# Encoder block with a mixture of experts: the last stage's row sums moved to TensorE, its one-hots to GpSimd

## Chip, cores and metric

One core of a Trainium2 chip runs the whole kernel. The metric is device microseconds of one execution, taken as the median of three runs. "us" below is microseconds and "span" is the time from the first to the last instruction in a profiled execution. PE is TensorE (the matrix engine), DVE is VectorE, ACT is ScalarE, POOL is GpSimd and SP is SyncE, which here only issues DMAs.

## What is computed

The block is a normalised input projection, two mixers (Fourier and state space), a gated output projection, and then a mixture of 64 experts with two experts for each of 2048 rows of 1024 numbers. Only the end of it matters for this change:

```python
def _rmsnorm(x, g):
    inv = lax.rsqrt(jnp.mean(x * x, axis=-1, keepdims=True) + RMS_EPS)
    return x * inv * g

# x: 2048 x 1024, after the two mixers
hn = _rmsnorm(x, ffn_norm_g)
# each row goes to two of 64 experts: a = silu(xb @ w_gate[e]) * (xb @ w_up[e]); y = (a @ w_down[e]) * weight
x = x + hier_moe(hn, ...)          # sum of the row's two weighted expert results
return _rmsnorm(x, final_norm_g)
```

All of it is float32. Products of large matrices are made of three products of a high and a low part in a reduced format (`fp32r`), so every weight block is first split into two parts `w_h` and `w_l`.

## The kernel before

The kernel goes through stages one after another; the expert loop (`stage_e`) takes 64 experts, one 128-row tile each, and the last stage (`stage_z`) puts the results together. In the expert loop ACT and DVE split each 128x2048 block of weights (L1685 and L1691), PE multiplies, and each expert's result rows are scattered by GpSimd to `y01` in memory. `y01` has two halves of 2048 rows: half 0 holds the row's residual plus its first expert's result, half 1 its second expert's result. The results of the last two experts, 62 and 63, are not scattered. They stay on the chip as pairs of parts in `r_last` (written by `last_result` at L1795, L53 and L54), and the last stage adds them into their rows by a product with a one-hot matrix: `oh` has a one where a row's number in the tile equals the number of a result row (`col`), so `oh` times the result places each result row where it belongs.

The last stage covers the 2048 rows in 16 tiles of 128 rows, in `steps`: seven steps of two tiles and then two steps of one. For step `n`, `load` brings the two halves of `y01` into `ys[n, 0]` and `ys[n, 1]` on SP's queue (L1992). The stage then does this for every step:

- `add(n)`, L2012: GpSimd adds the two halves into `ys[n, 0]`, 128x2048 numbers in one instruction.
- `onehot(n)`, L2020: DVE makes the step's one-hots, two for each tile, one for each of the last two experts.
- `products(n)`, L2032: PE multiplies one-hots and result parts into two PSUM buffers of 128x512 per tile (pools `pgu` with four buffers and `py` with two, so three tiles fit): eight products a tile.
- `total(n)`, L2041 and L2042: DVE adds PSUM to `ys[n, 0]`, two instructions a tile; ACT squares the sum and accumulates the row's mean square.
- `rsqrt_steps`, L72 to L78: DVE scales (L72), GpSimd takes the power -1/2 (L73), and DVE refines it in four small instructions (L75 to L78).
- `final(n)`, L2048: DVE multiplies the sum by the inverse root and by the weight vector `gf`, one instruction a tile.
- `store(n)`, L2052: the result goes out, on GpSimd's queue for the first seven steps and on ACT's for the last two.

These are written in a loop with `products` one step ahead and `onehot` and `add` two steps ahead. No planner moves them: each engine runs its instructions in the order in which the code issues them, and an instruction waits for what it reads. `stage_z` is a generator: `stage_e` runs it up to its first `yield` in expert 62 and up to its second in expert 63, and up to the third after `down(63)`, the last expert's products (L59 to L61 into `py`), and ahead of `last_result(63)`; then it runs to the end.

Of the kernel before, what the change touches and what calls it, by code (L numbers as in the profile page):

```python
# [11 lines left out]
F32 = mybir.dt.float32  # L12
F32R = mybir.dt.float32r
I32 = mybir.dt.int32
AF = mybir.ActivationFunctionType
OP = mybir.AluOpType
# [3 lines left out]
P = 128  # L20
# [16 lines left out]
class K:  # L37
# [1935 lines left out]
    def stage_z(self):  # L1973

        nc, tc, i, mr = self.nc, self.tc, self.i, self.mr
        V, A, SP = nc.vector, nc.scalar, nc.sync
        E = 64
        steps = [(2 * n, 2) for n in range(7)] + [(14, 1), (15, 1)]
        N = len(steps)
        rows = lambda v, t, m: v[t * P : (t + m) * P].rearrange("(t p) d -> p t d", p=P)  # L1980
        ys, tiles, marks, ohs, pss = {}, {}, {}, {}, {}

        def load(n, k, eng):
            t, m = steps[n]
            if n in late:
                tiles[n, k] = self.ewp.tile([P, 2048], F32R, name=("w_h", "w_l")[k]).bitcast(F32)
            elif k < m:
                tiles[n, k], mark = self.raw_tile()
                marks.setdefault(n, []).append(mark)
            both = tiles[n, min(k, m - 1)].rearrange("p (t d) -> p t d", t=2)  # L1990
            ys[n, k] = both if m == 2 else both[:, k : k + 1]
            eng.dma_start(ys[n, k], rows(self.y01, 16 * k + t, m))  # L1992


        late = (5, 6)
        self.ring = self.full
        self.loads += [(lambda eng, n=n, k=k: load(n, k, eng), n not in late and k < steps[n][1]) for n in (0, 1, 2, 3, 4, 7) + late + (8,) for k in range(2)]
        self.load_end = len(self.loads) - 6

        col = mr.tile([P, 2, 16], F32, name="z_col")  # L2000
        idx = mr.tile([P, 2], F32, name="z_idx")
        V.tensor_scalar(idx, self.tb[:, E - 2 : E, 0], 2.0 * T, None, op0=OP.add)
        for q in range(2):
            V.scalar_tensor_tensor(col[:, q], self.iota[:, 0:16], -128.0, idx[:, q : q + 1].to_broadcast([P, 16]), op0=OP.mult, op1=OP.add)
        yield
        g = mr.tile([P, D], F32, name="gf", tag="hn")
        A.dma_start(g, i["final_norm_g"].broadcast_to([P, D]))
        yield

        def add(n):  # L2010
            if n < N:
                nc.gpsimd.tensor_tensor(out=ys[n, 0], in0=ys[n, 0], in1=ys[n, 1], op=OP.add)  # L2012

        def onehot(n):
            if n < N:
                t0, m = steps[n]
                ohs[n] = mr.tile([P, 2, 2, P], F32R, name=f"oh{n % 2}", tag=("hnT", "rw")[n % 2])
                for t in range(m):
                    for q in range(2):
                        V.tensor_scalar(ohs[n][:, t, q], self.iota, col[:, q, t0 + t : t0 + t + 1], None, op0=OP.is_equal)  # L2020

        def products(n):
            if n < N:
                for t in range(steps[n][1]):
                    pool, name = ((self.pgu, "pgu"), (self.pgu, "pgu"), (self.py, "py"))[len(pss) % 3]
                    pss[n, t] = [pool.tile([P, 512], F32, name=name) for h in range(2)]
                    for h in range(2):
                        hs = slice(512 * h, 512 * h + 512)
                        for q in range(2):
                            w = self.r_last[q - 2]  # L2030
                            for k, part in enumerate((w.h, w.l)):
                                nc.tensor.matmul(pss[n, t][h], ohs[n][:, t, q], part[:, hs], start=q + k == 0, stop=q + k == 2)  # L2032

        def total(n):
            y0, y1 = ys[n, 0], ys[n, 1]
            m = steps[n][1]
            ss = mr.tile([P, 2], F32, name="ssz", bufs=2)
            for t in range(m):
                for h in range(2):
                    hs = slice(512 * h, 512 * h + 512)  # L2040
                    V.tensor_tensor(out=y0[:, t, hs], in0=y0[:, t, hs], in1=pss[n, t][h], op=OP.add)  # L2041
                A.activation(y1[:, t], y0[:, t], AF.Square, accum_out=ss[:, t : t + 1])  # L2042
            return self.rsqrt_steps(ss[:, :m], m, *(mr.tile([P, m], F32, name=f"z{m}{n % 2}{q}") for q in "vyt"))

        def final(n, inv):
            y0, y1 = ys[n, 0], ys[n, 1]
            for t in range(steps[n][1]):
                V.scalar_tensor_tensor(y1[:, t], y0[:, t], inv[:, t : t + 1], g, op0=OP.mult, op1=OP.mult)  # L2048

        def store(n):  # L2050
            t0, m = steps[n]
            (nc.gpsimd if n < N - 2 else A).dma_start(rows(self.out, t0, m), ys[n, 1])  # L2052
            for m in marks.get(n, []):
                m[0] = True
            self.load_more()

        add(0)
        add(1)
        onehot(0)
        onehot(1)  # L2060
        yield
        self.load_end = len(self.loads)
        self.load_more()
        products(0)
        for n in range(N):
            products(n + 1)
            norm = total(n)
            if n:
                final(n - 1, inv)
            next(norm)  # L2070
            if n:
                store(n - 1)
            onehot(n + 2)
            add(n + 2)
            inv = next(norm)
        final(N - 1, inv)
        store(N - 1)


# [114 lines left out]
```

## Time and profile before

| what | us |
|---|---|
| median of three runs (2478.20 to 2482.54) | 2479.97 |
| the profiled execution | 2482.89 |
| its span | 2481.1 |
| the last expert's last product starts | 2384.35 |
| first addition of the last stage (L2041) starts | 2389.53 |

The profile is of one execution, 2.9 us above the median. The span of 2481.1 us is 1.8 us less than that execution's whole time. Times in the trace count from the start of the span, so the last stage is the stretch from about 2384 to 2481 us. A timeline row gives the start, the duration, the engine, the line of the kernel and "out<-in" with the names of the tiles; what stands in brackets is the engine's idle time before it and what ended it. Rows of small instructions that follow each other are merged with a count. Busy time of DVE includes time in which an instruction has begun but does not get on. "PEclk" is the clock granted to TensorE, as a share of 2.4 GHz: 1.00 is 2.4 GHz, 0.50 is 1.2 GHz, and a number between is a stretch that held both.

### The profile page before, as it was taken

Reading aid. Unit: us, or ns where it says so; the run is one execution under the profiler, and the core shown is the slowest. Engines: PE = TensorE matmul, PEld = TensorE weight load, DVE = VectorE, ACT = ScalarE, POOL = GpSimd, SP = SyncE. Lnnn points to the kernel's source line nnn. Section 1 sums busy time; section 2 is a strip of 40 time slices with the busy share of each in tenths; the row PEclk is TensorE's granted clock in tenths of the full one; section 3 lists DMA queues with packets and bytes.
Section 4 is the critical chain, followed back from the end, with each engine's and each line's share of the span. In section 5 each row is a group of like instructions: output and inputs, shape, how many; then the busy total and the mean of one; then the engine's idle time right before and its main releaser. Section 6 shows DMA issues by size and latency. Waiting matters only on the chain.

```text
span 2481.1 us, 32354 instructions
## 1 busy us (share of the span) xinstructions
PE 2304.4 (93%) x11770; PEld 1914.1 (77%) x11770; DVE 2111.1 (85%) x2944; ACT 1367.5 (55%) x1635; POOL 722.2 (29%) x354
## 2 busy tenths in 40 slices
PE   6998999999998999996999979999999999999974
PEld 6997778878787999984877768777777777777752
DVE  7786779888936556556999979999999999999998
ACT  4443245544533222223777758777777777777721
POOL 2224500000002010012333231232246556556434
PEclk9999999999999999997999989999999999999985
DMA  5566644364445333346999979999999999989982
GB/s 192 179 192 214 237 129 157 111 229 128 132 123 197 114 108 95 110 142 234 334 342 365 375 270 393 362 352 351 361 356 361 367 365 365 384 318 360 361 316 118
DMA packets 201404, 632.70 MB, mean 255 GB/s; under 512 B 28998, under 2 KB 99656, under 8 KB 150556
## 3 DMA queue, kind: packets, MB, share of 16 engines
q1 hardware_dynamic: 170668, 571.01, 63.7%
q0 software_dynamic: 23104, 47.06, 5.1%
q10 hardware_dynamic: 7472, 12.55, 1.6%
q8 instruction: 93, 1.52, 0.3%
q14 instruction: 67, 0.55, 0.1%
HBM read 560.75 MB, written 103.32 MB: 268 GB/s over the span
## 4 chain that ended last, share of the span: by engine, by line
DVE 41%; PE 36%; issue 12%; DMA 6%; ACT 3%; POOL 1%; SPq 1%; DVEq 0%; POOLq 0%; ACTq 0%
DVE w_l L1691 19%; PE pg L59 3%; PE pg L61 3%; PE pg L60 3%; DVE xT_l L1770 3%; DVE xn L1829 2%; PE po L59 2%; PE pgu L60 2%; PE po L61 2%; PE po L60 2%; PE pgu L61 2%; PE pgu L59 2%; DVE xg L1795 2%; DVE a L1869 2%; ACT w_h L1685 2%
## 5 line engine op out<-in xcount | busy, mean ns | idle before, releaser
L1691 DVE TENSOR_TENSOR w_l<-raw,w_h 128x2048 fp32r<-128x2048 f32 x384 | 875.4, 2319 | 11.9 <-ACT w_h L1685 11.9
L1685 ACT CAST w_h<-raw 128x2048 fp32r<-128x2048 f32 x384 | 726.3, 1906 | 205.4 <-PE pgu L61 164.4
L59 PE MATMUL pgu<-w_h,xT_h 128*128 128x512 f32 x1024 | 406.7, 397 | 14.4 <-issue 14.4
L60 PE MATMUL pgu<-w_l,xT_h 128*128 128x512 f32 x1024 | 406.9, 397 | 4.6 <-DVE w_l L1691 2.3
L61 PE MATMUL pgu<-w_h,xT_l 128*128 128x512 f32 x1024 | 401.8, 392 | 0.0
L1758 POOL DMA_INDIRECT y<-xg,ix x42 | 180.7, 4302 | 423.3 <-DVE aT_l L1770 386.2
L60 PEld LDWEIGHTS pgu<-w_l,xT_h 128*128 128x128 f32 x1024 | 193.8, 189 | 65.3 <-DVE w_l L1691 28.2
L59 PEld LDWEIGHTS pgu<-w_h,xT_h 128*128 128x128 f32 x1024 | 193.7, 189 | 53.5 <-issue 14.6
L61 PEld LDWEIGHTS pgu<-w_h,xT_l 128*128 128x128 f32 x1024 | 193.4, 189 | 39.2 <-DVE xT_l L1770 0.2
L59 PE MATMUL pg<-hk_h,wg_h 128*128 128x512 f32 x512 | 206.6, 404 | 6.8 <-ACT gt_t L834 6.5
L59 PE MATMUL py<-w_h,aT_h 128*128 128x512 f32 x512 | 206.0, 402 | 4.0 <-ACT aT_h L1768 4.0
L61 PE MATMUL pg<-hk_h,wg_l 128*128 128x512 f32 x512 | 201.6, 394 | 1.8 <-DVE wg_l L54 1.8
L60 PE MATMUL pg<-hk_l,wg_h 128*128 128x512 f32 x512 | 201.0, 393 | 0.0
L61 PE MATMUL py<-w_h,aT_l 128*128 128x512 f32 x512 | 200.9, 392 | 0.0
L60 PE MATMUL py<-w_l,aT_h 128*128 128x512 f32 x512 | 200.9, 392 | 0.0
L1758 POOL DMA_INDIRECT y<-x_l,ix x22 | 94.4, 4292 | 235.6 <-DVE aT_l L1770 228.2
L1753 POOL DMA_INDIRECT xg<-x,ix x42 | 156.9, 3735 | 12.8 <-issue 12.8
L59 PEld LDWEIGHTS pg<-hk_h,wg_h 128*128 128x128 f32 x512 | 97.2, 190 | 27.9 <-ACT gt_t L834 7.1
L61 PEld LDWEIGHTS pg<-hk_h,wg_l 128*128 128x128 f32 x512 | 97.1, 190 | 23.6 <-DVE wg_l L54 2.7
L54 POOL TENSOR_TENSOR w_out_l<-raw_hn,w_out_h 128x1024 fp32r<-128x1024 f32 x1 | 2.4, 2377 | 386.6 <-DMA raw_x_l<-in_w_out 386.6
L59 PEld LDWEIGHTS py<-w_h,aT_h 128*128 128x128 f32 x512 | 97.0, 189 | 22.5 <-ACT aT_h L1768 4.2
L61 PEld LDWEIGHTS py<-w_h,aT_l 128*128 128x128 f32 x512 | 96.7, 189 | 20.8 <-DVE aT_l L1770 0.3
(564 smaller groups left out, 5042.0 us busy)
## 6 DMA issues: line engine op xcount, KB each, us to landing
raw<-in_w_e SPq DMA_DIRECT2D x376, 1024.0 KB
wg_raw<-in_w_g SPq DMA_DIRECT2D x32, 512.0 KB
raw<-y SPq DMA_DIRECT2D x10, 1024.0 KB
hTh<-hp_h SPq DMA_DIRECT2D x8, 1024.0 KB
hTl<-hp_l SPq DMA_DIRECT2D x8, 1024.0 KB
hk_h<-hTh SPq DMA_DIRECT2D x16, 512.0 KB
hk_l<-hTl SPq DMA_DIRECT2D x16, 512.0 KB
yf<-yt SPq DMA_DIRECT2D x16, 512.0 KB
```

What stands on the lines that cost most here:

```text
L54: (eng or nc.vector).tensor_tensor(out=dst.l, in0=src, in1=dst.h.bitcast(F32), op=OP.subtract)
L59: mm(out, a.h, b.h, start=start, stop=False)
L60: mm(out, a.h, b.l, start=False, stop=False)
L61: mm(out, a.l, b.h, start=False, stop=stop)
L1685: self.nc.scalar.copy(self.ws[n].h, self.raws[n][0])
L1691: self.nc.vector.tensor_tensor(out=w.l, in0=raw, in1=w.h.bitcast(F32), op=OP.subtract)
L1753: self.nc.gpsimd.indirect_dma_start(out=xg, out_offset=None, in_=self.x2, in_offset=bass.IndirectOffsetOnAxis(ap=ix[:, e, 0:1], axis=0), b ...
L1758: self.nc.gpsimd.indirect_dma_start(out=self.y01, out_offset=bass.IndirectOffsetOnAxis(ap=ix[:, e, 1:2], axis=0), in_=r, in_offset=None, b ...
L1770: self.nc.vector.tensor_tensor(out=xT.l[:, k0 : k0 + 4], in0=ps, in1=xT.h[:, k0 : k0 + 4].bitcast(F32), op=OP.subtract)
L1795: self.nc.vector.scalar_tensor_tensor(x[:, ns], yo[n], tb[:, e, 2:3], x[:, ns], op0=OP.mult, op1=OP.add)
L1829: V.scalar_tensor_tensor(xn[s], xg, tb[:, s, 3:4], self.g2, op0=OP.mult, op1=OP.mult)
L1869: at(0.1, lambda: V.tensor_tensor(out=a[s], in0=a[s], in1=ps[s, 1], op=OP.mult))
```

## The change

The two halves of `y01` are no longer added by GpSimd. Half 1 goes into the same PSUM sum as the one-hot products, by a product of the identity matrix (`ident`, float32) with `ys[n, 1]`, so that `total` adds both at once. GpSimd makes the one-hots instead of DVE. PE's work is ordered by tiles (`u`, 16 of them) instead of steps: `first(u)` makes the two identity products and expert 62's four one-hot products, `rows_of(u, 1)` adds expert 63's four. For tiles 0 and 1 `first` stands ahead of `last_result(63)`; for tile 2 it stands behind it, and then come the rest of tiles 0, 1 and 2. In the loop PE's work for later tiles stands behind `total(n)`, up to three tiles ahead. There are three sets of one-hots instead of two; sets 1 and 2 live in the buffers of the last expert's input (`xT_h`, `xT_l`). All stores go out on SP's queue. The lines move down by 2 to 6 (L2041 becomes L2047, L2048 becomes L2054, L2032 becomes L2028 and L2037).

```diff
--- before.py
+++ after.py
@@ -2007,38 +2007,44 @@
         A.dma_start(g, i["final_norm_g"].broadcast_to([P, D]))
         yield
 
-        def add(n):
-            if n < N:
-                nc.gpsimd.tensor_tensor(out=ys[n, 0], in0=ys[n, 0], in1=ys[n, 1], op=OP.add)
+        tile_of = [(n, k) for n, (t0, m) in enumerate(steps) for k in range(m)]
+        U = len(tile_of)
 
         def onehot(n):
             if n < N:
                 t0, m = steps[n]
-                ohs[n] = mr.tile([P, 2, 2, P], F32R, name=f"oh{n % 2}", tag=("hnT", "rw")[n % 2])
+                pool, tag = ((mr, "hnT"), (self.ep1, "xT_h"), (self.ep1, "xT_l"))[n % 3]
+                ohs[n] = pool.tile([P, 2, 2, P], F32R, name=f"oh{n % 3}", tag=tag)
                 for t in range(m):
                     for q in range(2):
-                        V.tensor_scalar(ohs[n][:, t, q], self.iota, col[:, q, t0 + t : t0 + t + 1], None, op0=OP.is_equal)
-
-        def products(n):
-            if n < N:
-                for t in range(steps[n][1]):
-                    pool, name = ((self.pgu, "pgu"), (self.pgu, "pgu"), (self.py, "py"))[len(pss) % 3]
-                    pss[n, t] = [pool.tile([P, 512], F32, name=name) for h in range(2)]
-                    for h in range(2):
-                        hs = slice(512 * h, 512 * h + 512)
-                        for q in range(2):
-                            w = self.r_last[q - 2]
-                            for k, part in enumerate((w.h, w.l)):
-                                nc.tensor.matmul(pss[n, t][h], ohs[n][:, t, q], part[:, hs], start=q + k == 0, stop=q + k == 2)
+                        nc.gpsimd.tensor_scalar(ohs[n][:, t, q], self.iota, col[:, q, t0 + t : t0 + t + 1], None, op0=OP.is_equal)
+
+        def rows_of(u, q):
+
+            n, t = tile_of[u]
+            w = self.r_last[q - 2]
+            for h in range(2):
+                for k, part in enumerate((w.h, w.l)):
+                    nc.tensor.matmul(pss[u][h], ohs[n][:, t, q], part[:, 512 * h : 512 * h + 512], start=False, stop=q + k == 2)
+
+        def first(u):
+
+            if u < U:
+                n, t = tile_of[u]
+                pool, name = ((self.pgu, "pgu"), (self.pgu, "pgu"), (self.py, "py"))[u % 3]
+                pss[u] = [pool.tile([P, 512], F32, name=name) for h in range(2)]
+                for h in range(2):
+                    nc.tensor.matmul(pss[u][h], self.ident, ys[n, 1][:, t, 512 * h : 512 * h + 512], start=True, stop=False)
+                rows_of(u, 0)
 
         def total(n):
+            t0, m = steps[n]
             y0, y1 = ys[n, 0], ys[n, 1]
-            m = steps[n][1]
             ss = mr.tile([P, 2], F32, name="ssz", bufs=2)
             for t in range(m):
                 for h in range(2):
                     hs = slice(512 * h, 512 * h + 512)
-                    V.tensor_tensor(out=y0[:, t, hs], in0=y0[:, t, hs], in1=pss[n, t][h], op=OP.add)
+                    V.tensor_tensor(out=y0[:, t, hs], in0=y0[:, t, hs], in1=pss[t0 + t][h], op=OP.add)
                 A.activation(y1[:, t], y0[:, t], AF.Square, accum_out=ss[:, t : t + 1])
             return self.rsqrt_steps(ss[:, :m], m, *(mr.tile([P, m], F32, name=f"z{m}{n % 2}{q}") for q in "vyt"))
 
@@ -2049,29 +2055,34 @@
 
         def store(n):
             t0, m = steps[n]
-            (nc.gpsimd if n < N - 2 else A).dma_start(rows(self.out, t0, m), ys[n, 1])
+            SP.dma_start(rows(self.out, t0, m), ys[n, 1])
             for m in marks.get(n, []):
                 m[0] = True
             self.load_more()
 
-        add(0)
-        add(1)
-        onehot(0)
-        onehot(1)
+        for n in range(3):
+            onehot(n)
+        first(0)
+        first(1)
         yield
         self.load_end = len(self.loads)
         self.load_more()
-        products(0)
+        first(2)
+        for u in range(3):
+            rows_of(u, 1)
+        done = 3
         for n in range(N):
-            products(n + 1)
             norm = total(n)
+            while done < min(U, steps[n][0] + steps[n][1] + 3):
+                first(done)
+                rows_of(done, 1)
+                done += 1
             if n:
                 final(n - 1, inv)
             next(norm)
             if n:
                 store(n - 1)
-            onehot(n + 2)
-            add(n + 2)
+            onehot(n + 3)
             inv = next(norm)
         final(N - 1, inv)
         store(N - 1)
```

On PE, at the end of the last expert and the begin of the last stage: `py` is the expert's output, `w_h_21234` and `w_l_21235` are expert 62's result, `w_h_21282` and `w_l_21283` expert 63's, and `raw` is a half of `y01`. Before:

```order
L61 MATMUL py_21245<-w_h_21193,aT_l_21228 128x512
L2032 MATMUL pgu_21298<-w_h_21234,oh0_21272 128x512
L2032 MATMUL pgu_21298<-w_l_21235,oh0_21272 128x512
L2032 MATMUL pgu_21298<-w_h_21282,oh0_21272 128x512
L2032 MATMUL pgu_21298<-w_l_21283,oh0_21272 128x512
L2032 MATMUL pgu_21299<-w_h_21234,oh0_21272 128x512
L2032 MATMUL pgu_21299<-w_l_21235,oh0_21272 128x512
L2032 MATMUL pgu_21299<-w_h_21282,oh0_21272 128x512
L2032 MATMUL pgu_21299<-w_l_21283,oh0_21272 128x512
L2032 MATMUL pgu_21308<-w_h_21234,oh0_21272 128x512
```

The third product waits for expert 63's result. With the change:

```order
L61 MATMUL py_21245<-w_h_21193,aT_l_21228 128x512
L2037 MATMUL pgu_21285<-raw_21138,ident_58 128x512
L2037 MATMUL pgu_21286<-raw_21138,ident_58 128x512
L2028 MATMUL pgu_21285<-w_h_21234,oh0_21270 128x512
L2028 MATMUL pgu_21285<-w_l_21235,oh0_21270 128x512
L2028 MATMUL pgu_21286<-w_h_21234,oh0_21270 128x512
L2028 MATMUL pgu_21286<-w_l_21235,oh0_21270 128x512
L2037 MATMUL pgu_21293<-raw_21138,ident_58 128x512
L2037 MATMUL pgu_21294<-raw_21138,ident_58 128x512
L2028 MATMUL pgu_21293<-w_h_21234,oh0_21270 128x512
L2028 MATMUL pgu_21293<-w_l_21235,oh0_21270 128x512
L2028 MATMUL pgu_21294<-w_h_21234,oh0_21270 128x512
```

These twelve products of tiles 0 and 1 stand ahead of the first that needs expert 63's result, and tile 2's six, not shown, follow them there; the identity products (L2037) are new.

On GpSimd, from the last scatter of the expert loop to the fourth step of the last stage (`oh` with a number is a set of one-hots, `z20y` and `z21y` are the power -1/2):

```order
-L2012 TENSOR_TENSOR raw<-raw 128x2048 x2
+L2020 TENSOR_SCALAR oh_21270<-iota,z_col 128x128 x4
+L2020 TENSOR_SCALAR oh_21275<-iota,z_col 128x128 x4
+L2020 TENSOR_SCALAR oh_21280<-iota,z_col 128x128 x4
 L73 TENSOR_TENSOR z20y<-z20v,mhalf 128x2
-L2012 TENSOR_TENSOR raw<-raw 128x2048
+L2020 TENSOR_SCALAR oh_21373<-iota,z_col 128x128 x4
 L73 TENSOR_TENSOR z21y<-z21v,mhalf 128x2
-L2052 DMA out<-raw 128x2x1024
-L2012 TENSOR_TENSOR raw<-raw 128x2048
+L2020 TENSOR_SCALAR oh_21424<-iota,z_col 128x128 x4
 L73 TENSOR_TENSOR z20y<-z20v,mhalf 128x2
```

The 128x2048 additions and the stores are gone from the queue; three sets of four one-hots stand at its front, and one set behind each power.

## Rows read from the trace of the kernel before

**Rows 1.** Page: shares of the last chain; its rows: start, us, what.

```profile
DVE 41%; PE 36%; issue 12%; DMA 6%; ACT 3%; POOL 1%; SPq 1%; DVEq 0%; POOLq 0%; ACTq 0%
...
2418.99 5.08 DVE z20t L76
```

**Rows 2.** VectorE from 2389 us: durations min/median/max; groups: busy us, mean ns.

```profile
L75 DVE TENSOR_TENSOR z20t<-z20y x4: 160/161/4510, 2396.6 to 2462.0; 128x2 f32<-128x2 f32 x4
...
L76 DVE TENSOR_TENSOR z20t<-z20t,z20v 128x2 f32<-128x2 f32 x4 | 13.2, 3291 | 0.1
L76 DVE TENSOR_TENSOR z21t<-z21t,z21v 128x2 f32<-128x2 f32 x3 | 13.1, 4357 | 0.1
```

**Rows 3.** Timeline of one step, VectorE and GpSimd: start us, us, line.

```profile
2415.39 2.48 DVE L2048 SCALAR_TENSOR_TENSOR raw<-raw,z21y,gf 128x1024 f32<-128x1024 f32 x2
2417.86 0.87 DVE L2020 TENSOR_SCALAR oh<-iota,z_col 128x128 fp32r<-128x128 f32 x4
...
2418.99 5.06 DVE L76 TENSOR_TENSOR z20t<-z20t,z20v 128x2 f32<-128x2 f32 x1
...
2418.03 0.73 POOL L73 TENSOR_TENSOR z20y<-z20v,mhalf 128x2 f32<-128x2 f32 x1 [5.37 <-DVE z20v L72]
...
2419.49 4.53 POOL L2012 TENSOR_TENSOR raw<-raw 128x2048 f32<-128x2048 f32 x1
```

**Rows 4.** Timeline, TensorE and VectorE: the stage's start, and its last total.

```profile
2384.58 0.39 PE L2032 MATMUL pgu<-w_h,oh 128*128 128x512 f32 x1
...
2386.55 1.40 DVE L1795 SCALAR_TENSOR_TENSOR xg<-py,tbm,xg 128x512 f32<-128x512 f32 x2
...
2389.53 0.69 DVE L2041 TENSOR_TENSOR raw<-raw,pgu 128x512 f32<-128x512 f32 x1 [0.21 <-PE pgu L2032]
...
2393.65 0.69 DVE L2041 TENSOR_TENSOR raw<-raw,pgu 128x512 f32<-128x512 f32 x1 [0.24 <-PE pgu L2032]
...
2470.50 1.28 DVE L2041 TENSOR_TENSOR raw<-raw,pgu 128x512 f32<-128x512 f32 x2
```

**Rows 5.** Timeline of TensorE: f32 products (351 us), one-hot products (2394, 2419).

```profile
351.48 1.07 PE L1053 MATMUL py<-hs,cy 128*128 128x256 f32 x4
352.39 0.60 PE L1050 MATMUL py<-u,toep 128*128 128x256 f32 x2
...
2394.62 0.40 PE L2032 MATMUL py<-w_l,oh 128*128 128x512 f32 x1
2394.86 0.40 PE L2032 MATMUL py<-w_h,oh 128*128 128x512 f32 x1
...
2419.21 0.63 PE L2032 MATMUL py<-w_h,oh 128*128 128x512 f32 x1
2419.64 0.63 PE L2032 MATMUL py<-w_l,oh 128*128 128x512 f32 x1
```

**Rows 6.** Stretches: length; PE, PEld, DVE, ACT, POOL busy; PEclk; DMA share; GB/s.

```profile
351.00:356.00 5.00, 5.00 (x37) 3.83 (x36) 4.93 (x9) 0.59 (x1) 0.00 (x0) 1.00 0.68 210
...
768.00:780.00 12.00, 7.56 (x58) 6.75 (x56) 9.94 (x14) 4.70 (x8) 7.49 (x3) 1.00 0.76 245
...
2388.00:2399.00 11.00, 10.72 (x38) 8.20 (x38) 7.42 (x12) 2.90 (x5) 3.19 (x2) 0.84 1.02 409
...
2413.70:2418.00 4.30, 3.78 (x8) 2.48 (x8) 4.30 (x7) 2.21 (x4) 0.00 (x0) 0.50 0.11 45
```

**Rows 7.** Groups of GpSimd instructions by shape: busy us, mean ns.

```profile
masks.py:199 POOL TENSOR_SCALAR_AFFINE_SELECT ident<-ident 128x128 f32<-128x128 f32 x1 | 0.3, 288 | 0.0
...
L605 POOL TENSOR_TENSOR rot<-sga,sgb 128x128 f32<-128x128 f32 x2 | 0.9, 462 | 0.0
...
L73 POOL TENSOR_TENSOR z20y<-z20v,mhalf 128x2 f32<-128x2 f32 x4 | 2.9, 728 | 26.0 <-DVE z20v L72 26.0
```

**Rows 8.** Timeline of VectorE ahead of the last expert's second half.

```profile
2366.44 4.49 DVE L1691 TENSOR_TENSOR w_l<-raw,w_h 128x2048 fp32r<-128x2048 f32 x2
```

## The prediction

> **What bounds the kernel now.** I read the page's chain of waits first. VectorE has the largest share of it, and near its end the chain shows an oddity: one instruction on a 128x2 tile, L76, that takes 5 us [rows 1]. The durations of such instructions come next. Of the four L75 three take 0.16 us and one takes 4.51, and the seven L76 take 13.2 + 13.1 = 26.3 us together [rows 2]. The timeline of one step says why: L76 stands from 2418.99 to 2424.05, and GpSimd's addition L2012 stands from 2419.49 to 2424.02 [rows 3]. So a tiny VectorE instruction is held while GpSimd adds 128x2048 numbers, once in each of steps 0 to 6. Behind it on VectorE stand the rest of the root, the next step's four additions and the `final` of the step, so nothing moves meanwhile. From the first addition of the stage to its last but one total are 2470.50 - 2389.53 = 80.97 us [rows 4]; some 30 of these are held time.
>
> Then the resources. TensorE is no bound: in a stretch inside a step its clock is at 0.50 (1.2 GHz), and the DMA engines are 0.11 busy there [rows 6]. Only at the stage's start is it dense (10.72 of 11 us) [rows 6], and there VectorE's first four additions wait for it: the first starts at 2389.53 and the fourth ends at 2394.34, 4.81 us, where four unheld ones take 2 x 1.28 = 2.56 [rows 4].
>
> **Part by part.** All terms are against the profiled span of 2481.1 us. That execution took 2482.89 us, 2.9 above the median of 2479.97; I apply the sum to the median.
>
> (a) *The GpSimd additions go.* The held time is 26.3 + 4.51 = 30.8 us in eight instructions (seven L76, one L75), and each of them unheld takes 0.16 [rows 2]. Gain 30.8 - 1.3 = **29.5 us**. What is late next in a step is the chain on VectorE itself: additions, `final`, root. It has no second cover to lose, since the loads of a step (2 x 1.05 MB, 5.1 us at the 409 GB/s of the stage's start [rows 6]) are shorter than a step without the hold, 50 us over seven and a half pairs of tiles = 6.7 us.
>
> (b) *The first addition comes later.* Before, PE does two one-hot products at 2384.58, waits for `last_result`, and the first addition starts at 2389.53 [rows 4]. Now PE has `first(0)`, `first(1)` and `first(2)` ahead of expert 63's products of tile 0. An identity product is f32. The trace has f32 products only as records of 256 columns; the four of L1053 take 352.39 - 351.48 = 0.91 us [rows 5], so I count 0.91 us for 512 columns in two records, at full clock [rows 6]. A one-hot product takes 0.235 us at full clock (2394.62 to 2394.86) [rows 5]. One `first` is 2 x 0.91 + 4 x 0.235 = 2.76 us; three end at 2384.58 + 8.28 = 2392.86, two more one-hot products 0.47, and a product ends 0.16 after its successor starts (0.40 - 0.24) [rows 5]: 2393.5. Loss **4.0 us**. `last_result` does not set this: VectorE's last one-hots no longer stand ahead of L1795 at 2386.55 [rows 4], so it ends earlier.
>
> (c) *The next three additions stop waiting for PE*, because PE is then a tile or more ahead: 4.81 - 2.56, gain **2.3 us**.
>
> (d) *One-hots on GpSimd, in the loop.* Twenty stand there: four each in steps 0 to 3, two each in steps 4 and 5. They stand right behind GpSimd's power L73, so they start as VectorE starts L75 to L78, the very place that was held. No row shows a one-hot on GpSimd. Nearest by size and by one input is the 128x128 affine select, 0.288 us; two inputs of that size took 0.462 [rows 7]. I take 0.35, nearer to the former since a one-hot has one large input and a column. Whether it holds VectorE is bounded by two rows: the addition did hold L76 for all of its 4.53 us, while VectorE's four one-hots ran in 0.87 us beside a power of 0.73 that ran at that time on GpSimd, unheld [rows 3]. So the price lies between 0 and 20 x 0.462 = 9.2. A one-hot reads a whole tile as the addition did and a power does not, so I take the full hold: 20 x 0.35 = loss **7.0 us**. Taking one-hots off VectorE gains nothing in the loop: those four stand where VectorE waits for the power anyway (2417.86 to 2418.73, the power ends at 2418.76) [rows 3].
>
> The Trainium skill, SBUF — State Buffer, section "Who interferes with whom", says that a VectorE instruction with two SBUF inputs and a GpSimd instruction that reads SBUF exclude each other for the whole instruction. The trace of L76 agrees, 5.06 us beside 4.53. By this rule the hold costs as in (d); by the row of the power it would cost nothing, and the sum would be 7.0 us better.
>
> (e) *One-hots on GpSimd, ahead.* Twelve are made in expert 63, among VectorE's weight splits L1691, 4.49 us for two [rows 8], which have two inputs as well and follow each other closely. An instruction can only be held where GpSimd begins first, which is between two long splits; so bounds 0 and 12 x 0.462 = 5.5, and I take a third, 4 x 0.35 = loss **1.4 us**.
>
> (f) *At nothing.* The 32 f32 products cost PE 32 x 0.91 = 29 us, beside VectorE: sixteen tiles at 2 x 0.91 + 8 x 0.235 = 3.70 are 59.2 us from 2384.58, and from the last total at 2470.50 to the end are 10.6 us [rows 4], so PE alone would end the span at 2454.4, 7 us below my sum. PE runs on three tiles of PSUM and so waits for `total` three tiles back, which VectorE does every 3.5 us or so; it keeps no long gap, and at 768 to 780 it was granted 1.00 while 7.56 of 12 us busy [rows 6]. The stores: seven issues leave GpSimd's queue and nine join SP's. Behind store n on SP stand only the two loads of step 8, which wait for the same `final(0)` as store 0 does, since they go to the buffers that it frees. The DMA engines have room [rows 6].
>
> Sum: -29.5 + 4.0 - 2.3 + 7.0 + 1.4 = **-19.4 us**, span 2461.7, time 2479.97 - 19.4 = **2460.6 us**.
>
> The Trainium skill, GPSIMD Engine Reference, section "4.1 Engine selection", speaks against one half of the change: elementwise work on a tile belongs on VectorE. The trace agrees, as VectorE's four one-hots lay hidden beside the power; left there, (d) and (e) would be nothing and the sum -27.8 us. Nothing run so far shows that version.
>
> **Rivals.**
>
> *A, one-hots on GpSimd hold nothing.* For it: the unheld row of the power [rows 3]. Against it: L76. VectorE's sum is then -27.8, below PE's own end at 2454.4, so PE sets it: -26.7 and **2453.3 us**.
>
> *B, they hold at the top price.* All 32 at 0.462: 14.8 in place of 8.4, so -13.0 and **2467.0 us**.
>
> *C, slower: TensorE stays at half clock.* At 0.50 a one-hot product takes 0.43 us (2419.21 to 2419.64) [rows 5] and an identity product twice 0.91. A tile is then 2 x 1.82 + 8 x 0.43 = 7.08 us, sixteen 113.3, the end 2384.58 + 113.3 + 10.6 = 2508.5 us, +27.4: **2507.4 us**. It decides from a tile of (2481.1 - 10.6 - 2384.6) / 16 = 5.37 us on, a mean clock of about 0.69. For it: 0.50 inside the steps of before, and 0.84 even in the dense stretch of the stage's start, where a pause of PE ahead of expert 63's result went before [rows 6]. Against it: PE now has no such pause and 7.4 us of work in a step of about 7.8, and the stretch at 768 was granted 1.00 with less.
>
> *D, the gain is taken back by another wait.* With steps shorter by 4 us, the loads of the next step or the stores on one queue become what VectorE waits for, to the old pace: about **2480 us**. For it: the 1.02 share of the DMA engines at the start [rows 6]. Against it: 0.11 inside a step, and 5.1 us of load for 6.7 us of step. The change would then not do what it says.
>
> *E, a one-hot on GpSimd costs as much as a power*, 0.728 [rows 7]: 32 x 0.73 = 23.4 in place of 8.4, -4.4 and **2475.6 us**.
>
> **How the numbers follow.** Forecast 0.55, with its own range 2455 to 2466; A 0.16, B 0.17, E 0.04, D 0.02, C 0.06. The range reaches to A and B and the sizes around them: 2452 to 2471, which leaves out C, D and E and some tails. About 0.2% (5 us) is what a measurement of this kernel can tell from no change; faster by over that is the forecast with A and B, 0.88; within it D and E, 0.06; slower C, 0.06.
>
> **What would show it.** In the profile after, L75 to L78 take 0.16 us, or up to 0.5 beside a one-hot (a), (d), and no instruction of 128x2 stands for 4 us. The one-hots on GpSimd take 0.3 to 0.46 us each. The first addition starts at 2393 to 2395 (b). A step of two tiles takes 7 to 8 us. The granted clock is 1.00 from 2385 to 2443 with PE busy nearly all the time. The prediction is wrong if the clock is near 0.5 there, if identity products take more than 1 us, if a GpSimd one-hot takes over 0.7 us, or if VectorE's additions wait for a DMA or for PE in each step.

## The result, and the profile after

The changed kernel takes 2454.89 us (median of four runs, 2447.98 to 2456.76), the kernel before 2481.26 in the runs beside it; the ratio is 0.9886, with an interval of 0.9873 to 0.9899 (the quotient of the two medians, 0.9894, lies in it). So it is 26.4 us faster where 19.4 were forecast. 2454.89 lies in the range of 2452 to 2471, just under the forecast's own range of 2455 to 2466, near rival A's 2453.3 and 5.7 us from the forecast's 2460.6.

The profiled execution has a span of 2454.9 us against 2481.1, 26.2 us less. Three views of it show where they went. First the groups of VectorE's small instructions from 2389 us on (busy us, mean ns), which answer to [rows 2], and GpSimd's one-hots:

```profile
L76 DVE TENSOR_TENSOR z20t<-z20t,z20v 128x2 f32<-128x2 f32 x4 | 0.6, 162 | 0.1
L75 DVE TENSOR_TENSOR z20t<-z20y 128x2 f32<-128x2 f32 x4 | 0.6, 161 | 3.4 <-POOL z20y L73 3.4
L76 DVE TENSOR_TENSOR z21t<-z21t,z21v 128x2 f32<-128x2 f32 x3 | 0.5, 163 | 0.1
...
L2020 POOL TENSOR_SCALAR oh<-iota,z_col 128x128 fp32r<-128x128 f32 x20 | 11.8, 603 | 0.0
```

The 26.3 us of L76 are 1.1, and none of them stands for more than 0.17 us. Second, busy time by stretch (length; PE, PEld, DVE, ACT, POOL; PEclk; DMA share; GB/s), which answers to [rows 6]:

```profile
2376.50:2382.00 5.50, 5.50 (x13) 4.19 (x14) 0.75 (x2) 0.00 (x0) 3.42 (x6) 0.50 1.02 408
2385.00:2442.00 57.00, 57.00 (x193) 35.90 (x191) 41.81 (x82) 18.02 (x31) 16.79 (x27) 1.00 0.74 296
```

From the first identity product to the last one-hot product TensorE is busy without a gap, 57.00 of 57.00 us, at 1.00 (2.4 GHz); VectorE has 41.81. Third, the end of the chain of waits in order of time (start, us, what):

```profile
2385.03 1.72 PE pgu L2037 x4
2386.75 0.93 PE pgu L2028 x4
...
2431.53 1.72 PE pgu L2037 x4
2433.25 1.42 PE pgu L2028 x6
2434.69 0.49 DVE w_h L2047
...
2449.15 1.28 DVE raw L2054
```

It runs along TensorE from the begin of the last stage to the second tile of step 6, and only then along VectorE, where before one L76 alone was a piece of 5.08 us [rows 1]. So the stage is now set by TensorE: 14 tiles of 3.58 us, and then VectorE's way to the end. In VectorE's timeline (start, us, idle time before it) this shows from step 4 on: the additions of the second tile wait for TensorE, by 0.17, 0.43 and 0.45 us in steps 4 to 6, 1.05 us together. The first and the last addition stand here too:

```profile
2393.48 2.48 DVE L2047 TENSOR_TENSOR raw<-raw,pgu 128x512 f32<-128x512 f32 x4 [6.28 <-PE pgu L2028]
...
2420.37 1.29 DVE L2047 TENSOR_TENSOR raw<-raw,pgu 128x512 f32<-128x512 f32 x2 [0.17 <-PE pgu L2028]
...
2434.69 1.29 DVE L2047 TENSOR_TENSOR w_h<-w_h,pgu 128x512 f32<-128x512 f32 x2 [0.45 <-PE pgu L2028]
...
2445.01 1.28 DVE L2047 TENSOR_TENSOR raw<-raw,pgu 128x512 f32<-128x512 f32 x2
```

The difference of the spans, piece by piece (before, after, in us; the first product is the first one-hot product before, and the first identity product after):

| piece | before | after | difference |
|---|---|---|---|
| start of the span to the first product | 2384.58 | 2384.87 | +0.29 |
| first product to the first addition | 4.95 | 8.61 | +3.66 |
| first addition to the last total | 80.97 | 51.53 | -29.44 |
| last total to the end | 10.6 | 9.9 | -0.7 |

### The profile page after: what moved, and what is told of

The parts are those of the page before. It is cut to its first block, busy times and chain, and to the rows that moved or that the text cites. A ratio compares the mean times of both kernels' runs of the same rounds, so it can differ in the third digit from the quotient of the medians.

```text
span 2454.9 us, 32486 instructions
## 1 busy us (share of the span) xinstructions
PE 2313.0 (94%) x11834; PEld 1918.7 (78%) x11834; DVE 2067.9 (84%) x2912; ACT 1368.0 (56%) x1635; POOL 782.6 (32%) x370
## 4 chain that ended last, share of the span: by engine, by line
DVE 42%; PE 38%; issue 12%; DMA 5%; ACT 2%; SPq 1%; POOL 0%; DVEq 0%; POOLq 0%; ACTq 0%
DVE w_l L1691 22%; PE pg L59 4%; PE pg L61 4%; PE pg L60 4%; DVE xn L1829 3%; DVE xT_l L1770 3%; PE po L59 2%; PE po L61 2%; PE po L60 2%; DVE xg L1795 2%; DVE a L1869 2%; DMA raw<-in_w_e 2%; DVE a L1840 1%; DVE aT_l L1770 1%; PE pso L60 1%
## 5 line engine op out<-in xcount | busy, mean ns | idle before, releaser
L1691 DVE TENSOR_TENSOR w_l<-raw,w_h 128x2048 fp32r<-128x2048 f32 x384 | 868.9, 2293 | 12.0 <-ACT w_h L1685 12.0
L1758 POOL DMA_INDIRECT y<-xg,ix x42 | 211.3, 5031 | 373.3 <-DVE aT_l L1770 336.1
L1758 POOL DMA_INDIRECT y<-x_l,ix x22 | 114.8, 5219 | 210.5 <-DVE aT_l L1770 203.1
L1753 POOL DMA_INDIRECT xg<-x,ix x42 | 171.3, 4078 | 12.8 <-issue 12.8
```

The costliest lines, as they stand in the source:

```text
L1691: self.nc.vector.tensor_tensor(out=w.l, in0=raw, in1=w.h.bitcast(F32), op=OP.subtract)
L1753: self.nc.gpsimd.indirect_dma_start(out=xg, out_offset=None, in_=self.x2, in_offset=bass.IndirectOffsetOnAxis(ap=ix[:, e, 0:1], axis=0), b ...
L1758: self.nc.gpsimd.indirect_dma_start(out=self.y01, out_offset=bass.IndirectOffsetOnAxis(ap=ix[:, e, 1:2], axis=0), in_=r, in_offset=None, b ...
```

## Experiments

Executions of one kernel differ by some us ahead of the last stage: a second profile of the changed kernel has a span of 2449.3 us, yet 70.1 us from its first identity product (2379.22) to the end, as the first profile has 70.0. So beside each median stands this stretch of the profiled run, here called the stage, from the first product of the last stage to the end of the span; before it was 2481.1 - 2384.58 = 96.5.

| run | median | ratio to before, 95% interval | stage |
|---|---|---|---|
| changed kernel | 2454.89 | 0.9886, 0.9873 to 0.9899 | 70.0 |
| z_after, the same again | 2453.86 | 0.9891, 0.9874 to 0.9909 | 70.1 |
| z_id_only | 2456.94 | 0.9905, 0.9885 to 0.9925 | 71.1 |
| z_oh_dve | 2454.10 | 0.9899, 0.9881 to 0.9917 | 70.1 |
| z_oh_twice | 2453.01 | 0.9891, 0.9873 to 0.9910 | 70.3 |
| z_pool_add | one run, 2455.65 | none | 74.1 |
| z_id_half | 2451.78 | 0.9875, 0.9857 to 0.9893 | 66.2 |
| z_order | 2457.16 | 0.9896, 0.9880 to 0.9912 | 70.0 |
| z_stores | 2457.55 | 0.9894, 0.9875 to 0.9914 | 70.8 |
| z_early2 | 2450.80 | 0.9872, 0.9853 to 0.9891 | 70.1 |

### The identity products alone

The kernel before, with nothing but the addition moved (for comparison, all else of the change is left out; in the edits, dots stand for lines not shown):

```diff
-                nc.gpsimd.tensor_tensor(out=ys[n, 0], in0=ys[n, 0], in1=ys[n, 1], op=OP.add)
+                pass
...
+                        nc.tensor.matmul(pss[n, t][h], self.ident, ys[n, 1][:, t, hs], start=True, stop=False)
...
-                                nc.tensor.matmul(pss[n, t][h], ohs[n][:, t, q], part[:, hs], start=q + k == 0, stop=q + k == 2)
+                                nc.tensor.matmul(pss[n, t][h], ohs[n][:, t, q], part[:, hs], start=False, stop=q + k == 2)
```

> The kernel before with one edit: GpSimd's addition goes, and an identity product on TensorE stands at the head of each PSUM sum. One-hots stay on VectorE, products stay in steps, stores stay on GpSimd and ScalarE. Theory 1 (the held time was all of it, and then TensorE's dense row of products, 3.58 us a tile, sets the end): 24 to 28 us faster than before, 2453 to 2457, no 128x2 instruction over 0.4 us, TensorE busy nearly without a gap over 2388 to 2443. Rival (the other parts, one-hots on GpSimd and products ahead of the last expert, carry a share): at least 4 us slower than the changed kernel, that is 2459 or more.

Measured: 2456.94 us, and 71.1 us for the stage, so 25.4 of the 26.5 us that the whole change takes off the stage. The mean durations of L76 and the stretch in which TensorE is dense:

```profile
L76 DVE TENSOR_TENSOR z20t<-z20t,z20v 128x2 f32<-128x2 f32 x4 | 0.6, 161 | 0.1
L76 DVE TENSOR_TENSOR z21t<-z21t,z21v 128x2 f32<-128x2 f32 x3 | 0.5, 161 | 0.1
```

```profile
2393.00:2443.00 50.00, 50.00 (x170) 31.60 (x168) 41.47 (x98) 14.98 (x26) 9.22 (x13) 1.00 0.71 283
```

Theory 1 holds in its mechanism: no 128x2 instruction stands for more than 0.4 us, and TensorE is busy for 50.00 of 50.00 us. Its gain was a little too high: against the kernel before, measured beside it at 2479.77, the median is 22.8 us less, where 24 to 28 were expected. The rival falls: 2456.94 is 2 us above the changed kernel and not 4, and the stage is 1 us longer. What the rest of the change adds to the stage is about 1 us, and 0.6 of it lies at the very end (10.5 us from the last total to the end, where the changed kernel has 9.9). In this kernel 2.65 us of the 25.4 come ahead of the first addition, which starts 2.30 us after the first product in place of 4.95; the likely reason stands below, at the end of "What holds VectorE".

### Who makes the one-hots

Two runs: VectorE makes them again, and GpSimd makes those of the loop twice.

```diff
-                        nc.gpsimd.tensor_scalar(ohs[n][:, t, q], self.iota, col[:, q, t0 + t : t0 + t + 1], None, op0=OP.is_equal)
+                        V.tensor_scalar(ohs[n][:, t, q], self.iota, col[:, q, t0 + t : t0 + t + 1], None, op0=OP.is_equal)
```

> The changed kernel with its one-hots made by VectorE again. Theory 1 (a one-hot on GpSimd holds VectorE by 0.2 us a step at most, and TensorE sets the pace): within 1.5 us of the changed kernel, L75 to L78 together 0.75 us from start to end in place of 0.93. Rival, as the prediction had it (a one-hot holds VectorE for its whole length, now 0.59 us): up to 20 x 0.59 = 11.8 us faster in the loop.

```diff
-                for t in range(m):
+                for t in [t for t in range(m) for _ in range(2 if n > 2 else 1)]:
```

> The changed kernel with the twenty one-hots of the loop made twice each by GpSimd, the same values again. Theory 1 (they hold next to nothing): 0 to 2 us slower than the changed kernel; GpSimd is busy for 0.72 + 8 x 0.59 = 5.4 us of a step of 6.6. Rival (each holds VectorE for its length): 20 x 0.59 = 11.8 us slower.

Measured: 70.1 and 70.3 us for the stage against 70.0; medians 2454.10 and 2453.01. Both rivals, which go by a full hold of 11.8 us, fall. The stage alone can't tell a delay of VectorE of about 1 us, since TensorE sets the pace. How little a one-hot on GpSimd holds is read from VectorE's timeline (start, us) of one step, of the changed kernel and then of z_oh_dve:

```profile
2404.82 0.16 DVE L75 TENSOR_TENSOR z21t<-z21y 128x2 f32<-128x2 f32 x1 [0.84 <-POOL z21y L73]
2405.02 0.16 DVE L76 TENSOR_TENSOR z21t<-z21t,z21v 128x2 f32<-128x2 f32 x1
2405.22 0.20 DVE L77 TENSOR_SCALAR z21t<-z21t 128x2 f32<-128x2 f32 x1
2405.45 0.30 DVE L78 TENSOR_TENSOR z21y<-z21y,z21t 128x2 f32<-128x2 f32 x1
```

```profile
2402.55 0.16 DVE L75 TENSOR_TENSOR z21t<-z21y 128x2 f32<-128x2 f32 x1
2402.74 0.16 DVE L76 TENSOR_TENSOR z21t<-z21t,z21v 128x2 f32<-128x2 f32 x1
2402.94 0.17 DVE L77 TENSOR_SCALAR z21t<-z21t 128x2 f32<-128x2 f32 x1
2403.14 0.16 DVE L78 TENSOR_TENSOR z21y<-z21y,z21t 128x2 f32<-128x2 f32 x1
```

From L75's start to L78's end are 0.93 us beside GpSimd's one-hots and 0.75 without them, so 0.18 us a step and 1.1 us in the six steps that have them. With twice as many, L75 to L78 still take 0.93 us. VectorE's steps 1 to 3 take 7.0 us in place of 6.6, because the next power now stands behind the one-hots on GpSimd (VectorE waits 1.12 us for it in place of 0.84) and the two `final` instructions take 2.59 in place of 2.47. The stage is still 70.3: TensorE needs 7.16 us a step anyway.

### What holds VectorE

One more GpSimd instruction in each of steps 0 to 6, of two operands in the even ones and of one in the odd ones:

```diff
             next(norm)
+            if n < 7:
+                spare = mr.tile([P, 512], F32, name="spare", tag="rw")
+                if n % 2 == 0:
+                    nc.gpsimd.tensor_tensor(out=spare, in0=g[:, 0:512], in1=g[:, 512:1024], op=OP.add)
+                else:
+                    nc.gpsimd.tensor_scalar(spare, g[:, 0:512], col[:, 0, 0:1], None, op0=OP.is_equal)
```

> The changed kernel with one more GpSimd instruction behind the power in each of steps 0 to 6, its result unused: in even steps an addition of two SBUF operands of 128x512, in odd steps a comparison of one SBUF operand of 128x512 with a column. Theory 1 (two operands hold VectorE, one does not): in even steps one of L75 to L78 stands for about a quarter of the old 4.5 us, 1.1 us; in odd steps all stay under 0.35. Rival a (any GpSimd instruction that is long enough holds it): both kinds of step show one of about the extra instruction's length. Rival b (a hold needs an instruction of several us): neither does. The time moves by 4 x 1.1 us at most.

Measured, in the timeline of GpSimd and VectorE, an even step (2407 us) and the odd one ahead of it (2400 us):

```profile
2400.89 1.58 POOL L2088 TENSOR_SCALAR spare<-gf,z_col 128x512 f32<-128x512 f32 x1
...
2407.68 1.30 POOL L2086 TENSOR_TENSOR spare<-gf 128x512 f32<-128x512 f32 x1
```

```profile
2400.93 0.16 DVE L75 TENSOR_TENSOR z21t<-z21y 128x2 f32<-128x2 f32 x1 [0.85 <-POOL z21y L73]
2401.13 0.46 DVE L76 TENSOR_TENSOR z21t<-z21t,z21v 128x2 f32<-128x2 f32 x1
...
2407.75 1.25 DVE L75 TENSOR_TENSOR z20t<-z20y 128x2 f32<-128x2 f32 x1 [0.84 <-POOL z20y L73]
2409.03 0.30 DVE L76 TENSOR_TENSOR z20t<-z20t,z20v 128x2 f32<-128x2 f32 x1
```

The addition of two operands, 1.30 us, holds L75 for 1.25 us, all of it. The comparison of one operand is longer, 1.58 us, and L75, L76, L77 and L78 all run inside of it; one of them takes 0.46, 0.30 more than unheld. All four even steps have a hold of L75 (1.21 to 1.28 us), and all three odd steps have the 0.46. So length is not what decides (rival a falls), nor is a short hold excluded (rival b falls); the form is. What in the form it is, the run doesn't tell: the two instructions differ in the number of tiles that they read, and also in their operation and kind (TENSOR_TENSOR, TENSOR_SCALAR). Theory 1 was off in one point: the 0.46 of L76 in odd steps is over the 0.35 that it allowed, so the one-operand form does hold a little. The stage grew by 4.1 us: the holds add 4 x 1.1 + 3 x 0.3 = 5.3 us to VectorE's row, and the 1.05 us that it spent waiting for TensorE take up part of them.

The kernel before has another row of this. VectorE's eight one-hots ahead of the stage, each a comparison of one tile with a column, ran beside GpSimd's first two additions, and then the same eight in z_id_only, where GpSimd adds nothing:

```profile
2376.94 9.69 DVE L2020 TENSOR_SCALAR oh<-iota,z_col 128x128 fp32r<-128x128 f32 x8
...
2376.13 4.71 POOL L2012 TENSOR_TENSOR raw<-raw 128x2048 f32<-128x2048 f32 x1 [11.91 <-ACT w_h L53]
2381.31 4.65 POOL L2012 TENSOR_TENSOR raw<-raw 128x2048 f32<-128x2048 f32 x1 [0.46 <-DMA raw<-y]
```

```profile
2380.14 1.65 DVE L2020 TENSOR_SCALAR oh<-iota,z_col 128x128 fp32r<-128x128 f32 x8
```

They take 9.69 us in place of 1.65, and two of them 3.98 and 4.61. So GpSimd's addition holds VectorE instructions of one tile as well, and so `last_result` (L1795), which stands behind them on VectorE, began only at 2386.55, 2 us after the stage's first product; in z_id_only it began 0.5 us ahead of that product. The prediction counted only the holds inside the steps.

### TensorE's share of the pace

The identity product of columns 512 to 1023 is left out:

```diff
-                    nc.tensor.matmul(pss[u][h], ohs[n][:, t, q], part[:, 512 * h : 512 * h + 512], start=False, stop=q + k == 2)
+                    nc.tensor.matmul(pss[u][h], ohs[n][:, t, q], part[:, 512 * h : 512 * h + 512], start=h == 1 and q + k == 0, stop=q + k == 2)
...
-                for h in range(2):
-                    nc.tensor.matmul(pss[u][h], self.ident, ys[n, 1][:, t, 512 * h : 512 * h + 512], start=True, stop=False)
+                nc.tensor.matmul(pss[u][0], self.ident, ys[n, 1][:, t, 0:512], start=True, stop=False)
```

> The changed kernel without the identity product of columns 512 to 1023 of each tile, so half 1 of y01 is left out of half of the result. A tile costs TensorE 2.7 us in place of 3.58. Theory 1 (TensorE sets the pace, VectorE is close behind at 6.6 us a step): first addition 2.6 us earlier, steps 4 to 6 go from 7.15 to 6.6 us, 3 to 4 us faster than the changed kernel. Rival (as the prediction had it, VectorE alone sets the steps): 2.6 us faster, steps 4 to 6 as before. If TensorE's sum were all that counts: 16 x 0.85 = 13.6 us.

Measured: 66.2 us for the stage, 3.8 less. TensorE is busy for 38.60 of the 49.5 us from 2390.5 to 2440, and no addition of steps 1 to 6 waits for it. Steps 4 to 6 take 6.5 to 6.6 us; this is where steps 4 and 5 begin:

```profile
2415.91 1.27 DVE L2046 TENSOR_TENSOR raw<-raw,py 128x512 f32<-128x512 f32 x2
...
2422.54 1.27 DVE L2046 TENSOR_TENSOR w_h<-w_h,pgu 128x512 f32<-128x512 f32 x2
```

Theory 1 holds. Of the 3.8 us, 2.6 come from the first addition, which starts 6.0 us after the first product in place of 8.6, and about 1.2 from the waits for TensorE that are gone. So TensorE sets the pace of the changed kernel, but once VectorE has begun it is only about 1 us behind: the two rows are nearly even. The sum of TensorE's savings, 13.6 us, is not had, since VectorE's 6.6 us a step take over.

### The first addition earlier

Only tile 0's `first` stands ahead of expert 63's result:

```diff
         first(0)
-        first(1)
         yield
...
-        first(2)
         for u in range(3):
+            if u:
+                first(u)
             rows_of(u, 1)
```

> The changed kernel with TensorE's first three tiles in another order: only tile 0's identity and expert 62 products stand ahead of expert 63's result, then tile 0 is finished, then tile 1, then tile 2. Theory 1 (TensorE's dense row sets the end, and term (b), the first addition 4 us late, is given back by it only in part): first addition at about 3.5 us after the first identity product in place of 8.6, VectorE waits for TensorE in the early steps instead, the last total starts at TensorE's end, 2 to 3 us faster than the changed kernel. Rival 1 (VectorE sets the pace all along): 5 us faster. Rival 2 (TensorE's end is all that counts): 0 to 0.5 us.

Measured: the first addition starts 3.3 us after the first identity product in place of 8.6, and the stage takes 70.0 us as before; the median is 2457.16 beside 2453.86 for the changed kernel (z_after), and in the two profiled executions the whole difference lies ahead of the stage, which starts at 2385.26 and 2379.22. Theory 1 falls and rival 2 holds. VectorE's timeline in z_order shows why:

```profile
2388.59 1.28 DVE L2047 TENSOR_TENSOR raw<-raw,pgu 128x512 f32<-128x512 f32 x2 [0.99 <-PE pgu L2028]
2392.17 1.29 DVE L2047 TENSOR_TENSOR raw<-raw,pgu 128x512 f32<-128x512 f32 x2 [2.30 <-PE pgu L2028]
...
2406.46 1.28 DVE L2047 TENSOR_TENSOR raw<-raw,py 128x512 f32<-128x512 f32 x2 [0.42 <-PE py L2028]
2413.63 1.28 DVE L2047 TENSOR_TENSOR raw<-raw,pgu 128x512 f32<-128x512 f32 x2 [0.45 <-PE pgu L2028]
...
2435.09 1.28 DVE L2047 TENSOR_TENSOR w_h<-w_h,pgu 128x512 f32<-128x512 f32 x2 [0.45 <-PE pgu L2028]
```

Its additions wait for TensorE in each of steps 0 to 6, 7.17 us apart (2406.46 to 2413.63). In the changed kernel VectorE begins 5.3 us later and catches up at 6.6 us a step until step 4. Either way the second tile of step 6 comes from TensorE at the same time, and what follows is the same.

### Where the stores are issued

```diff
-            SP.dma_start(rows(self.out, t0, m), ys[n, 1])
+            (nc.gpsimd if n < N - 2 else A).dma_start(rows(self.out, t0, m), ys[n, 1])
```

> The changed kernel with the stores where they were, seven on GpSimd's queue and two on ScalarE's. Theory 1 (the queue of a store is off the path): 70 us from the first identity product to the end, within 0.5. Rival (the last store on ScalarE's queue ends later: before, 10.6 us lay between the last total and the end, with the change 9.9): 0.5 to 0.7 us longer at the very end and nothing elsewhere. Were GpSimd's seven issues of 0.77 us on the path between the powers: up to 5 us.

Measured: 70.8 us for the stage, 0.8 more, of which about 0.6 lie behind the start of the last `final` (2449.09 to 2455.4 against 2449.15 to 2454.9). The rival holds in size, by one profile of each kernel. The medians, 2457.55 and 2454.89, were not measured side by side and cannot tell 0.8 us.

### A version that starts the stage earlier

If TensorE's row sets the end, then only an earlier start of it helps. Ahead of the last expert's 24 products TensorE sits idle for 4.00 us and then runs at 0.50, as the first stretch above shows; it waits for `aT_h` on ScalarE, which stands behind expert 62's result, which stands on VectorE behind a weight split (L1691, 2371.68 to 2373.96):

```profile
2374.71 1.22 ACT L53 CAST w_h<-xg 128x512 fp32r<-128x512 f32 x2 [6.34 <-DVE xg L1795]
2375.83 0.58 ACT L1768 CAST aT_h<-pst 128x512 fp32r<-128x512 f32 x1
2376.47 0.79 PE L59 MATMUL py<-w_h,aT_h 128*128 128x512 f32 x1 [4.00 <-ACT aT_h L1768]
```

On top of z_order:

```diff
-            at(1.9, self.split_l, n + self.AHEAD)
+            at(1.9 if n + self.AHEAD + 1 < len(order) else 6.8, self.split_l, n + self.AHEAD)
...
-            result(s)
+            if s == E - 1:
+                result(s)
...
-                at(0.1, last_result, s - 1)
+                at(0.1, result, s - 1)
             turned(a[s], 4, "aT", aT, s)
+            if s == E - 1:
+                at(2.0, last_result, s - 1)
```

> The kernel of the run before, and ahead of the last expert's second half VectorE takes the sums of expert 62 and the low part of the last expert's aT ahead of the last weight split, ScalarE the high part of aT ahead of expert 62's result parts. Theory 1: TensorE's gap of 4.0 us ahead of the last 24 products shrinks to 1 to 1.5, the clock stays at 1.00 and the products take 0.23 us each in place of 0.43 for the first fourteen: 4 to 6 us faster than the run before. Rival (the loads of the last stage, at 410 GB/s from 2370 us on, set the pace when the stage starts earlier): 0 to 2 us, and TensorE or VectorE waits for a load.

Measured: 2450.80 us, 6.4 us less than z_order and 3.1 less than the changed kernel (z_after), all measured side by side; the interval of its ratio, 0.9853 to 0.9891, overlaps with that of the changed kernel. The trace is clearer. TensorE's idle time, and the stretch of the 24 products:

```profile
2373.38 0.50 PE L59 MATMUL py<-w_h,aT_h 128*128 128x512 f32 x1 [0.73 <-ACT aT_h L1768]
```

```profile
2373.40:2379.00 5.60, 5.60 (x23) 4.33 (x24) 4.39 (x5) 0.96 (x2) 5.60 (x6) 1.00 1.03 414
```

The gap is 0.73 us in place of 4.00 (1 to 1.5 expected), and the clock is 1.00 in place of 0.50. From the last expert's transposes (L1766, 2371.99) to the first identity product (2379.23) are 7.2 us, where the changed kernel has 2384.87 - 2371.81 = 13.1: 5.8 us gained, and the stage is 70.1 as ever. Against other profiles with the gap of 4.00 us, where this way takes 11.5 to 13.1 us, it is 4.3 to 5.9. The rival, loads that set the pace, falls.

## Why the prediction was right in sign and range, and short in size

- (a) Right in its mechanism: the held instructions are down to 0.16 us each, and z_id_only, which does little but take the addition off GpSimd, has 25.4 of the 26.5 us. Seven were held and not eight, as in the first step L75 was held and L76 took 0.16; the gain of 29.5 is the same. That the piece from the first addition to the last total shrank by 29.44 us is partly luck: the terms in it are -29.5, -2.3 of (c), +1.1 that (d) measured, and 1.05 of waits for TensorE.
- (b) and (c) Right as times, but not what the end hangs on. The first addition starts at 2393.48 (2393.5 forecast) and the first four take 2.48 us (2.56). But z_order moves the first addition by 5.3 us and the end not at all: starting VectorE earlier gains nothing once TensorE's row is the path. They could stand in the sum only because VectorE's row, begun at 2393.48, is within about 1 us of TensorE's.
- (d) This is the step that failed: the hold that a one-hot on GpSimd puts on VectorE. "A one-hot reads a whole tile as the addition did and a power does not, so I take the full hold" put 7.0 us there; 0.18 us a step and 1.1 us in all were measured. The duration was missed as well: 0.603 us for a one-hot, above both bounds, 0.288 and 0.462 [rows 7]; it didn't matter, since GpSimd has the time. z_pool_add shows what the row of L76 could not: GpSimd's addition of two tiles holds VectorE for all of its length, its comparison of one tile with a column hardly. The row of the power [rows 3] said less than it was taken for: VectorE's one-hots, which ran freely beside it, stood for 9.69 us beside the additions. The Trainium skill, SBUF — State Buffer, section "Who interferes with whom", says that a VectorE instruction with two SBUF inputs contends with any GpSimd instruction that reads SBUF; for two operands the run agrees (1.25 us beside 1.30), for one it doesn't (0.46 beside 1.58), and the measurement decides.
- (e) The first product of the stage started 0.29 us later, where 1.4 was forecast, and even this is less than what two runs of one kernel differ by there. The hold went the other way. GpSimd's twelve one-hots ahead take 1.31 us each on average and the longest 2.74 (shortest, median and longest in ns in the second row), beside VectorE's splits of 2.3 us:

```profile
L2020 POOL TENSOR_SCALAR oh<-iota,z_col 128x128 fp32r<-128x128 f32 x12 | 15.6, 1313 | 0.0
...
L2020 POOL TENSOR_SCALAR oh<-iota,z_col x12: 596/597/2736, 2364.4 to 2379.3; 128x128 fp32r<-128x128 f32 x12
```

- (f) "PE alone would end the span at 2454.4, 7 us below my sum" came out as a number, partly by luck: the span ended at 2454.9, but TensorE's tile takes 3.58 us (3.70 forecast), 1.9 us less over sixteen tiles, and the last total stands 2.9 us behind TensorE's end, for which nothing was counted. It was counted as cover because the sum had 8.4 us of holds in it. With most of these gone, the cover is the bound: rival A, given 0.16 and 2453.3 us, is nearly what happened. z_id_half confirms it from the other side. One of the signs of being wrong, additions that wait for TensorE in each step, came in steps 4 to 6.
- The second weighing, that one-hots belong on VectorE (the Trainium skill, GPSIMD Engine Reference, section "4.1 Engine selection"), would have made the sum -27.8. z_oh_dve has the same stage within 0.1 us, so where the one-hots are made changes nothing that can be measured here, as long as TensorE sets the pace.
- Rival C did not come: the clock is 1.00 from 2385 to 2442. Nor did D: no addition waits for a load.
- The stores on SP gave 0.7 to 0.8 us (the last piece of the table, z_stores), counted at nothing.

Taken together, 6.8 us lie between the sum of -19.4 and the -26.2 of the spans. By pieces they are about 1.1 from (e), 0.3 from (b), 0.7 from the end of the stage, and 4.6 from the first addition to the last total; these last are the 5.9 us that (d) had too much, less 1.05 of waits for TensorE and 0.2 unexplained. The rest of the sum was a list of VectorE's delays although the engine that ends last had changed. The better sum is TensorE's start, 14 tiles, and VectorE's way from there: 2384.87 + 14 x 3.58 + 10.0 (from the end of TensorE's tile 13, the fourteenth, to the last total) + 9.9 = 2454.9. It is made from the profile after, so it is an account of it and no forecast.

What stays open is why GpSimd's comparison of one tile holds VectorE for 0.30 us and its addition of two tiles for its whole length; the runs show that it is so, not how. Open is also why L76 stood from 0.50 us before the addition's record begins (2418.99 and 2419.49 [rows 3]); the store that GpSimd issues there is not the cause, as L76 takes 0.16 us beside it in z_id_only.

## What to carry to other kernels

When a sum comes within a few us of another engine's own row of work, forecast that engine's end and ask whether the terms above it are sure; here a term that was a guess (7.0 us) hid the bound. Where a tiny VectorE instruction stands for microseconds, look for a GpSimd instruction that runs for just that time; here it was an addition of two tiles. Once one engine was busy without a gap, starting the others earlier was worth nothing here (z_order), and its own start was worth all: 5.8 us by taking three of VectorE's instructions ahead of a weight split.

## What was not expected of the hardware

- GpSimd's one-hot of 128x128 takes 0.60 us, and its comparison of 128x512 with one operand 1.58, longer than its addition of two operands of that size, 1.30.
- Two identity products of f32 (128x512 each) take 1.31 us until the next product starts, and that next one has 0.63 to itself in place of 0.235: 1.70 us for two, 0.85 each, where 0.91 was counted:

```profile
2384.87 1.88 PE L2037 MATMUL pgu<-raw,ident 128*128 128x512 f32 x4
2386.18 0.79 PE L2028 MATMUL pgu<-w_h,oh 128*128 128x512 f32 x1
```

- A gap of 4.00 us on TensorE was followed by 0.50 of the clock for over 5 us of dense products; after a gap of 0.73 us at the same place the clock stayed at 1.00. The gap cost 3.3 us and the slow products about 2.5. The length of the slow stretch differs between executions: in nine profiles with that gap, six to fifteen products ran at 0.43 us each, for 1.0 to 2.6 us.
